# A hybrid decoder layer on one core: where the forget sums are loaded, where a unit's output is stored, when the last stick-breaking sums are reduced, and when the last rows are scaled and turned

## The chip, the core and the metric

The kernel runs on one core of a Trainium2 chip. The metric is the time of one execution on the device, in microseconds (us). The engines of the core are TensorE (PE in the profile, with its weight loads as PEld), VectorE (DVE), ScalarE (ACT), GpSimd (POOL) and SyncE (SP), which here does nothing but issue transfers. Each engine works through its own instructions in the order in which they stand. All data is float32.

## What is computed

One layer of a decoder with a sequence of 2048 and a width of 1024. The rows are normalised and modulated, projected once, and go through 16 heads of width 64: 8 of forgetting attention (FoX) and 8 of stick-breaking attention. Each head's output is normalised, all are projected back, and a gated MLP with a short causal convolution follows.

```python
def forgetting_attention(q, k, v, log_f):
    F = jnp.cumsum(log_f, axis=-1)
    ...
        s = jnp.einsum('bhqd,bhkd->bhqk', q_blk, k) * scale
        s = s + F_blk[..., None] - F[:, :, None, :]
        s = jnp.where(causal, s, -jnp.inf)
        return jnp.einsum('bhqk,bhkd->bhqd', jax.nn.softmax(s, axis=-1), v)

def stick_breaking_attention(q, k, v):
    ...
        log_one_minus_beta = jnp.where(strict, jax.nn.log_sigmoid(-z), 0.0)
        rest = lax.cumsum(log_one_minus_beta, axis=3, reverse=True) - log_one_minus_beta
        a = jnp.where(strict, jnp.exp(jax.nn.log_sigmoid(z) + rest), 0.0)
        return jnp.einsum('bhqk,bhkd->bhqd', a, v)

h = rms_norm(x, g_attn) * (1.0 + scale_a) + shift_a
proj = h @ w_in                       # q, k, v of FoX and of stick-breaking, forget logits
mix = concat([head_rms_norm(o_fox, g_out_fox), head_rms_norm(o_sb, g_out_sb)])
x = x + gate_a * (mix @ w_out)
h = rms_norm(x, g_mlp) * (1.0 + scale_m) + shift_m
u = causal_depthwise_conv(h @ w_up, conv_w, conv_b)
x = x + gate_m * ((silu(u_gate) * u_val) @ w_down)
return rms_norm(x, g_final)
```

## The kernel before

Every float32 operand of a matmul is split into a high and a low part, and each product is made of three matmuls (high by high, high by low, low by high). Most splits are a copy on ACT (L45) and a subtraction (L46) on DVE or, for some, on POOL.

**Units.** Attention is done in 32 units. A unit is a kind (stick-breaking `sb` or FoX `fox`), a pair of heads p from 0 to 3, and a block tb of 512 queries. The 16 units of stick-breaking come first, then the 16 of FoX, in both cases pair by pair and block by block. Inside a unit there are two halves of 256 queries (`j2`), and in each the two heads of the pair. A head makes its logits (L596, L597), turns them into weights, transposes the weights through PE (L606; the copies out are L610 on ACT and L611 on DVE), and multiplies them by V (L615). In stick-breaking the weights come from a scan on DVE (L636), in front of which POOL clears the part over the diagonal (L633).

**FoX and its forget sums.** `fox_head` (L657 to L685) adds the cumulated forget logarithms of the keys to the logits in an operation of DVE that also keeps the smallest value (L675); for the diagonal chunk POOL first makes a masked copy `Fd` (L672). ACT's Exp (L679) then makes the weights and their sum. The sums `Fb` of a head, spread to all partitions, are four tiles of 128 x 1024 for a pair of heads; `load_sums` (L648 to L655) loads them from memory through SP. It runs ahead of unit 14 for pair 0, and with block 0 of each later pair (L1040). The four tiles share four buffers, so a load waits until DVE has done with the sums of the pair before.

**A unit's output.** The parts of the output are added up in `oT` on DVE (L738). `head_var` (L707 to L726) squares each half on POOL (L711) and puts a reduction on a list; the reduction, two small matmuls (L716) and one or two small operations of DVE (L722, L724), is made 13 steps of the program later, by `tick`. At the end of the unit SP stores `oT` to memory, as `os` (L740). Where the program goes from stick-breaking to FoX, `tick(1 << 20)` makes all reductions that are left, since the pool `sx`, in which the squares lie, is closed there (L1036 to L1038).

**Work around the units.** The projections of later pairs are generators, woven into the units step by step. `proj` reads the normalised input `hs` back from memory, 512 KB a tile (L468, on SP), and accumulates on PE (L342, L413). SP also loads Q (L362), K (L363), V (L364) and the weights (L316), and a second generator works on the modulation of the MLP (L776 and following).

**The order.** The program is written in this woven order, and a scheduler then fixes the order of the instructions on each engine when the kernel is built. `tc.issue_after` keeps an instruction behind another one. On the chip, an engine whose next instruction has to wait holds up all that stand behind it.

**The start of the MLP.** The first pair of up-projections is `pair_first` (L1327 to L1345): in each round j it makes seven products (L1316). After round 1 it calls `finish_last` (L1390 to L1394), which finishes the last chunk of rows of the attention output: `scale` multiplies two tiles of 128 rows by their norm (L997, L999), and four `turn_rows` transpose them on PE (L1005, in the bank `bc`) and modulate and store them (ACT, L1013).

## Time and profile before

| | us |
|---|---|
| median of 3 runs | 2949.6 |
| lowest and highest run | 2947.95 and 2951.05 |
| the profiled execution | 2949.67 |
| its span, from the first to the last instruction | 2948.0 |
| PE busy | 2872.7 |
| DVE busy | 2187.3 |
| ACT busy | 1689.3 |
| POOL busy | 899.8 |

The last stick-breaking unit adds its last output at 875.4 us of the span and the last FoX unit at 1519.5; the output projection follows until about 1712, and the MLP to the end. A row of the timeline has the start, the length, the engine, the line and what is written and read; in square brackets stands for how long the engine was idle just before, and what ended it. A row of waits has the sum, the number and the longest. A row of windows has, for each engine, the busy time and the count of instructions, then the clock granted to PE as a share of the full one, the mean busy share of the 16 DMA engines, and GB/s. A row of a line has an operation's least, median and largest length in nanoseconds. An engine's name with a q is its queue, where transfers are issued.

### The profile page before, as it was taken

What the parts mean: (1) busy time and instruction counts of PE and PEld (TensorE: products, weight loads), DVE (VectorE), ACT (ScalarE), POOL (GpSimd) and SP (SyncE); (2) the same over time, 40 slices, a digit from 0 to 9 for tenths busy, and PEclk for the clock granted to TensorE, in tenths of its full rate; (3) what the DMA queues carried; (4) which work ended last, traced back from release to release, by engine and by line L of the source; (5) the groups of instructions that cost most, each with busy time, mean ns of one, the idle gap of its engine ahead of it and who ended that gap; (6) DMA issues with size and microseconds to landing.
All of it is one profiled execution on the core that took longest, in us unless ns stands there. A gap on an engine that the chain in (4) does not pass through costs nothing.

```text
span 2948.0 us, 45934 instructions
## 1 busy us (share of the span) xinstructions
PE 2872.7 (97%) x15772; PEld 2466.9 (84%) x15772; DVE 2187.3 (74%) x3464; ACT 1689.3 (57%) x3187; POOL 899.8 (31%) x967
## 2 busy tenths in 40 slices
PE   8999999999999999999999999999999999999998
PEld 7888898888988889888788788888788888888887
DVE  5787778877877657658843688888998888575576
ACT  5776767777776666658743554444444444543342
POOL 0431312243022423231213344444254543142200
PEclk8999999999999999999999999999999999999999
DMA  9749756867469794794537765554744444975654
GB/s 292 254 133 328 221 196 210 298 202 234 151 217 355 252 296 145 231 323 140 182 115 232 250 219 134 136 136 125 230 134 128 129 133 129 301 266 189 212 159 148
DMA packets 348346, 601.89 MB, mean 204 GB/s; under 512 B 34672, under 2 KB 178800, under 8 KB 348112
## 3 DMA queue, kind: packets, MB, share of 16 engines
q1 hardware_dynamic: 324208, 558.06, 57.5%
q0 software_dynamic: 10880, 20.97, 4.4%
q10 hardware_dynamic: 13024, 19.93, 1.9%
q8 instruction: 124, 2.03, 0.3%
q14 instruction: 110, 0.90, 0.1%
HBM read 420.77 MB, written 177.02 MB: 203 GB/s over the span
## 4 chain that ended last, share of the span: by engine, by line
PE 48%; DVE 2%; DMA 2%; issue 1%; ACT 1%; SPq 0%; POOL 0%; DVEq 0%; ACTq 0%; POOLq 0%
PE ps_o L1316 19%; PE ps_t L1316 7%; PE ps_o L1613 6%; PE ps_t L1613 3%; PE ps_bc L1613 3%; PE ps_o L912 3%; PE ps_pv L615 2%; PE ps_pt L606 1%; PE ps_bc L912 1%; PE ps_qk L596 1%; DMA r<-rstd 1%; PE ps_o L1608 1%; DVE op L46 1%; PE ps_qk L597 1%; DMA hm<-hf_m 1%
## 5 line engine op out<-in xcount | busy, mean ns | idle before, releaser
L1316 PE MATMUL ps_o<-op,wu 128*128 128x512 f32 x2592 | 608.3, 389 | 2.0 <-DVE snap L1367 1.5
L1316 PEld LDWEIGHTS ps_o<-op,wu 128*128 128x128 f32 x2592 | 486.1, 188 | 103.9 <-DVE snap L1367 1.9
L611 DVE TENSOR_TENSOR at<-ps_pt,at 128x512 fp32r<-128x512 f32 (+1 forms) x576 | 365.8, 651 | 99.3 <-ACT at L610 96.8
L636 DVE TENSOR_TENSOR_SCAN a<-r,a 128x512 f32<-128x512 f32 (+2 forms) x320 | 368.7, 1168 | 76.6 <-ACT a L631 40.8
L342 PE MATMUL ps_pj<-hp,w_qk 128*128 128x512 f32 x1512 | 408.4, 401 | 11.0 <-DMA hp<-hs 8.6
L615 PE MATMUL ps_pv<-at,V 128*128 128x256 f32 x2304 | 405.5, 293 | 11.7 <-DVE at L611 4.7
L610 ACT ACTIVATE at<-ps_pt 128x512 fp32r<-128x512 f32 (+1 forms) x576 | 319.3, 576 | 139.2 <-PE ps_pt L606 123.0
L615 PEld LDWEIGHTS ps_pv<-at,V 128*128 128x128 f32 x2304 | 335.5, 191 | 44.9 <-DVE at L611 13.6
L342 PEld LDWEIGHTS ps_pj<-hp,w_qk 128*128 128x128 f32 x1512 | 274.7, 189 | 66.9 <-DMA hp<-hs 11.3
L596 PE MATMUL ps_qk<-K,Q 128*128 128x512 f32 (+2 forms) x640 | 266.8, 418 | 9.9 <-ACT a L631 4.7
L45 ACT ACTIVATE wu<-wuraw 128x512 fp32r<-128x512 f32 x204 | 128.8, 632 | 250.2 <-PE ps_o L1316 194.2
L413 PE MATMUL ps_pj<-w_v,hp 128*128 128x256 f32 (+1 forms) x1536 | 239.9, 290 | 1.3 <-DVE hp L422 0.9
L597 PE MATMUL ps_qk<-K,Q 128*128 128x512 f32 (+2 forms) x640 | 237.1, 372 | 0.0
L1316 PE MATMUL ps_t<-op,wu 128*128 128x512 f32 x888 | 220.5, 389 | 0.6 <-DVE op L46 0.6
L413 PEld LDWEIGHTS ps_pj<-w_v,hp 128*128 128x128 f32 x1536 | 211.7, 191 | 10.2 <-DVE q L373 1.3
L630 ACT ACTIVATE r<-ps_qk 128x512 f32<-128x512 f32 (+2 forms) x320 | 173.0, 541 | 59.7 <-PE ps_qk L597 57.0
L46 DVE TENSOR_TENSOR wu<-wuraw,wu 128x512 fp32r<-128x512 f32 x204 | 191.2, 937 | 18.2 <-ACT wu L45 17.0
L1316 PEld LDWEIGHTS ps_t<-op,wu 128*128 128x128 f32 x888 | 166.6, 188 | 35.6 <-DVE op L46 1.1
L606 PE MATMUL ps_pt<-edge,a 128*128 128x128 f32 x1088 | 186.0, 275 | 7.9 <-DVE a L636 7.4
L1613 PE MATMUL ps_o<-op 128*128 128x512 f32 x840 | 191.5, 389 | 0.0
L679 ACT ACTIVATE p<-p,mn 128x128 f32<-128x128 f32 (+15 forms) x128 | 153.9, 1203 | 56.4 <-DVE mn L675 54.8
L1613 PEld LDWEIGHTS ps_o<-op 128*128 128x128 f32 x840 | 157.7, 188 | 32.7
(338 smaller groups left out, 5215.5 us busy)
## 6 DMA issues: line engine op xcount, KB each, us to landing
hp<-hs SPq DMA_DIRECT2D x224, 512.0 KB
wuraw<-in_w_up_dram SPq DMA_DIRECT2D x80, 512.0 KB
ra<-g SPq DMA_DIRECT2D x136, 256.0 KB
rb<-in_w_down_dram SPq DMA_DIRECT2D x108, 256.0 KB
g<-u SPq DMA_DIRECT2D x80, 256.0 KB
hs<-hp SPq DMA_DIRECT2D x32, 512.0 KB
hp<-in_w_ada_dram SPq DMA_DIRECT2D x32, 512.0 KB
qk_fox<-q SPq DMA_DIRECT2D x32, 512.0 KB
```

Source lines behind the costliest of these rows:

```text
L46: (lo_engine or nc.gpsimd).tensor_sub(lo, src, f(hi))
L342: nc.tensor.matmul(acc, w[kt][:, a, n], h[:, bb], start=kt == 0 and i == 0, stop=kt == KT - 1 and i == 2)
L413: nc.tensor.matmul(av[:, t * width:(t + 1) * width], hts[kt][:, a, tok], w[1][kt][:, bb, 0:width], start=kt == 0 and m == 0, stop=kt == KT ...
L596: nc.tensor.matmul(b[:, :cw], Q[:, hl, 0, qcols], K[:, hl, :cw], start=True, stop=False)
L597: marks.append(nc.tensor.matmul(b[:, :cw], Q[:, hl, 1, qcols], K[:, hl, :cw], start=False, stop=True).ins)
L606: nc.tensor.transpose(b[:, i * P:(i + 1) * P], blk(kts[kk], qi), ident)
L610: copies = [nc.scalar.activation(at[:, 0, lo:], b[:, lo:], AF.Copy).ins, nc.vector.tensor_sub(at[:, 1, lo:], b[:, lo:], f(at[:, 0, lo:])).ins]
L611: nc.vector.tensor_sub(at[:, 1, lo:], b[:, lo:], f(at[:, 0, lo:])).ins]
L615: m = nc.tensor.matmul(o[:, 0:2 * P], V[kt // 4][:, kt % 4, hl, :], rhs, start=first and kk == 0 and w == 0, stop=last and kk == 1 and w == 1)
L636: nc.vector.tensor_tensor_scan(rev, r[:, 0:need][:, ::-1], rev, 0.0 if right[qi] is None else right[qi][:, 0:1], ALU.mult, ALU.add)
L1316: nc.tensor.matmul(b, w[:, p, j], o[:, q], start=first and i == 0, stop=last and i == 2, skip_group_check=True)
L1613: nc.tensor.matmul(b, a[:, p, t * P:(t + 1) * P], w[:, q], start=first and i == 0, stop=last and i == 2, skip_group_check=True)
```

## The change

Four things change; the arithmetic stays the same.

1. **The sums of pairs 1 to 3 are loaded from ACT's queue**, head by head. `load_sums` takes a head and a queue. In the last unit of a pair, behind each head's last Exp, the two tiles of that head are issued for the next pair. So 12 of 16 loads go from SP to ACT; the first four stay on SP, ahead of unit 14.
2. **The outputs of 31 of 32 units are stored from POOL's queue**, right behind the second square; the last one stays on SP.
3. **The flush of the reductions ahead of FoX is gone.** The last stick-breaking unit puts its squares into another pool, and they are reduced 13 steps later, as all others.
4. **`finish_last` is called after each round:** after round 0 it scales, after round 2 it transposes and modulates. Both stood after round 1.

```diff
-    def load_sums(p):
-        sums = [[], []]
+    def load_sums(p, hl, queue=nc.sync):
+        sums = []
         for t in range(0, NTB, 2):
-            for h in range(2):
-                b = px.tile([P, D], F32, name="Fb", tag="xt", bufs=4)
-                nc.sync.dma_start(b, fs[2 * p + h:2 * p + h + 1, t * TB:(t + 2) * TB].to_broadcast([P, D]))
-                sums[h] += [b[:, 0:TB], b[:, TB:D]]
+            b = px.tile([P, D], F32, name="Fb", tag="xt", bufs=4)
+            queue.dma_start(b, fs[2 * p + hl:2 * p + hl + 1, t * TB:(t + 2) * TB].to_broadcast([P, D]))
+            sums += [b[:, 0:TB], b[:, TB:D]]
         return sums
...
-            nc.scalar.activation(a[:, 0:W], a[:, 0:W], AF.Exp, scale=-1.0, bias=mn, accum_out=ls[:, hl, qc + qi:qc + qi + 1])
+            e = nc.scalar.activation(a[:, 0:W], a[:, 0:W], AF.Exp, scale=-1.0, bias=mn,
+                                     accum_out=ls[:, hl, qc + qi:qc + qi + 1])
+            if qi and then is not None:
+                with tc.issue_after(e.ins):
+                    then()
...
-        last_unit = (kind, p, tb) == units[-1]
+        i = units.index((kind, p, tb))
+        last_unit = i == len(units) - 1
...
-            sq = (sx.tile([P, 2 * P], F32, name="sq", bufs=1) if kind == "sb" else
+            sq = (sx.tile([P, 2 * P], F32, name="sq", bufs=1) if kind == "sb" and i < 15 else
                   px.tile([P, TB], F32, name="sq", tag="z", bufs=2)[:, 0:2 * P])
...
+            if j2:
+                (nc.sync if last_unit else nc.gpsimd).dma_start(os_[mp][tb], oT)
...
+                    then = None
+                    if j2 and tb == NTB - 1 and p < 3:
+                        then = lambda hl=hl: sums_of.setdefault(p + 1, []).append(load_sums(p + 1, hl, nc.scalar))
+                    yield from fox_head(j, 2 * j2, hl, Q, K, V, o, Fbs[hl], ls, then)
...
-        nc.sync.dma_start(os_[mp][tb], oT)
...
         if u == ("fox", 0, 0):
-            tick(1 << 20)
             close_pool("sx")
...
-        if i == 14 or (kind == "fox" and tb == 0 and p):
-            Fbs = load_sums(p if kind == "fox" else 0)
+        if i == 14:
+            sums_of[0] = [load_sums(0, hl) for hl in range(2)]
+        if kind == "fox" and tb == 0:
+            Fbs = sums_of[p]
...
-            if j == 1 and after is not None:
-                after()
+            if after is not None:
+                after(j)
...
-    def finish_last():
-        rows_done(NU - 1, 1)
-        ends[NU - 1].scale()
-        for k2 in range(4):
-            turn_rows(NU - 1, k2, bank(psc, "bc", 2))
+    def finish_last(j):
+        if j == 0:
+            rows_done(NU - 1, 1)
+            ends[NU - 1].scale()
+        elif j == 2:
+            for k2 in range(4):
+                turn_rows(NU - 1, k2, bank(psc, "bc", 2))
```

The scheduler orders all of the program anew, so that many instructions of the first three stages stand a few rows earlier or later than before.

PE where stick-breaking goes over to FoX, before (`a` are the weights of stick-breaking, `at` their transposes, `sq` the squares, `p` the weights of FoX):

```order
L606 MATMUL ps_pt<-edge,a 128x128 x4
L615 MATMUL ps_pv<-at,V 128x256 x12
L716 MATMUL ps_pt<-headsel,sq 128x2 x2
L596 MATMUL ps_qk<-K,Q 128x256
L597 MATMUL ps_qk<-K,Q 128x256
L596 MATMUL ps_qk<-K,Q 128x256
L597 MATMUL ps_qk<-K,Q 128x256
L606 MATMUL ps_pt<-edge,p 128x128 x3
```

The same place with the change:

```order
L606 MATMUL ps_pt<-edge,a 128x128 x4
L615 MATMUL ps_pv<-at,V 128x256 x8
L596 MATMUL ps_qk<-K,Q 128x256
L597 MATMUL ps_qk<-K,Q 128x256
L596 MATMUL ps_qk<-K,Q 128x256
L597 MATMUL ps_qk<-K,Q 128x256
L606 MATMUL ps_pt<-edge,p 128x128
L615 MATMUL ps_pv<-at,V 128x256 x3
L606 MATMUL ps_pt<-edge,p 128x128 x2
L596 MATMUL ps_qk<-K,Q 128x384
L597 MATMUL ps_qk<-K,Q 128x384
```

The first logits of FoX now stand between the last products with V of stick-breaking. The two reductions of `sq` (L716, now L723) come 15 rows further on:

```order
L606 MATMUL ps_pt<-edge,p 128x128 x3
L615 MATMUL ps_pv<-at,V 128x256
L606 MATMUL ps_pt<-edge,p 128x128 x4
L615 MATMUL ps_pv<-at,V 128x256 x3
L723 MATMUL ps_pt<-headsel,sq 128x2 x2
L596 MATMUL ps_qk<-K,Q 128x512
```

They stand there behind six pairs of logits (L596 with L597) and the transposes of the first of them.

SP where the second pair of FoX heads goes over to the third, before:

```order
L362 DMA Q<-qk_fox_0_13205 64x1024 x4
L740 DMA os_2_98<-oT 128x512
L653 DMA Fb<-fs 128x1024 x2
L363 DMA K<-qk_fox_1_14178 64x512 x4
L363 DMA K<-qk_fox_2_14948 64x512
L653 DMA Fb<-fs 128x1024
L363 DMA K<-qk_fox_2_14948 64x512
L362 DMA Q<-qk_fox_1_14178 64x1024
L653 DMA Fb<-fs 128x1024
L362 DMA Q<-qk_fox_1_14178 64x1024 x3
```

The same place with the change:

```order
L362 DMA Q<-qk_fox_0_13213 64x1024 x4
L316 DMA raw_qk<-in_w_in_dram 128x2x128
L363 DMA K<-qk_fox_1_14178 64x512 x4
L363 DMA K<-qk_fox_2_14948 64x512 x3
L362 DMA Q<-qk_fox_1_14178 64x1024 x4
L805 DMA gate_m<-hp 128x1024
L363 DMA K<-qk_fox_2_14948 64x512
L468 DMA hp<-hs_7_91 128x1024
```

The store and the four loads of sums are gone from SP. On ACT the loads for the first head of the third pair stand behind the Exp (L678, before L679) of 2048 columns:

```order
L678 ACTIVATE p,ls<-p,mn 128x1920
L610 ACTIVATE at<-ps_pt 128x512 x3
L678 ACTIVATE p,ls<-p,mn 128x2048
L652 DMA Fb<-fs 128x1024
L609 ACTIVATE at<-edge 128x2x128
L652 DMA Fb<-fs 128x1024
L610 ACTIVATE at<-ps_pt 128x384
L610 ACTIVATE at<-ps_pt 128x512 x2
```

Behind them stand the copies out of the transposes (L610). No transfer stands between these rows on ACT before the change.

More of the change, by code (lines that the diff above doesn't have):

```diff
@@ L688 @@
     deferred = []
+    sums_of = {}
     marks = []
@@ L734, in attend @@
                 else:
-                    yield from fox_head(j, 2 * j2, hl, Q, K, V, o, Fbs[hl], ls)
+                    then = None
+                    if j2 and tb == NTB - 1 and p < 3:
+                        then = lambda hl=hl: sums_of.setdefault(p + 1, []).append(load_sums(p + 1, hl, nc.scalar))
+                    yield from fox_head(j, 2 * j2, hl, Q, K, V, o, Fbs[hl], ls, then)
                 o2 = sb.tile([HD, 2 * P], F32, name="o2", bufs=2)
```

2 lines of the change are left out of this document (1 added, 1 removed).

## The prediction

> **What bounds the kernel now.** I read the page first (busy shares), then the windows by stage, the chain's releasers by PE's waits, SP's waits, and last the timelines at the places these name. The windows are cut where the stages end: units of stick-breaking until 875 us, FoX units until 1520, the output projection until 1712, then the MLP.
>
> ```profile
> PE 2872.7 (97%) x15772; PEld 2466.9 (84%) x15772; DVE 2187.3 (74%) x3464; ACT 1689.3 (57%) x3187; POOL 899.8 (31%) x967
> core 0: us, PE busy (x) PEld busy (x) DVE busy (x) ACT busy (x) POOL busy (x), PEclk, DMA share, GB/s
> 117.00:875.00 758.00, 733.92 (x4814) 655.36 (x4813) 603.23 (x792) 553.37 (x1194) 209.66 (x256) 0.99 0.66 221
> 875.00:1520.00 645.00, 626.63 (x4102) 558.11 (x4103) 442.69 (x1136) 424.94 (x811) 182.49 (x259) 0.99 0.68 228
> 1520.00:1712.00 192.00, 187.67 (x865) 152.56 (x864) 95.94 (x159) 90.50 (x190) 53.61 (x60) 0.98 0.69 227
> 1712.00:2520.00 808.00, 805.34 (x3553) 665.73 (x3552) 702.03 (x816) 385.06 (x531) 361.15 (x319) 1.00 0.55 149
> ```
>
> TensorE sets the time: it is busy for 2872.7 of 2948.0 us. The change lies between 117 and about 1705 us, and PE's order of work is unchanged after that. In the first three stages PE is idle for 24.1 + 18.4 + 4.3 = 46.8 us (length less busy, row by row). No rearrangement that leaves the matmuls alone can win more than this and what a throttled clock adds. PE's waits from 117 to 1712 us say what they are:
>
> ```profile
> engine line waited for: us in total, times, longest us
> PE ps_pj L342 <- DMA hp<-hs: 8.6, 6, 3.6
> PE ps_pt L606 <- DVE a L636: 5.7, 12, 1.2
> PE ps_qk L596 <- ACT a L631: 4.7, 6, 1.9
> PE ps_pv L615 <- DVE at L611: 4.7, 12, 0.8
> PE ps_pt L716 <- POOL sq L711: 1.6, 1, 1.6
> PE ps_bc L1005 <- DVE x1u L999: 0.2, 1, 0.2
> ```
>
> The largest is a load: a projection (L342) waits for the normalised input `hs`, read back from memory. The chains inside a head (L606, L596, L615) keep the same distances in the new order, so I leave them at nothing. The loads are issued by SP, whose instructions run in order, and SP itself stands at:
>
> ```profile
> SPq L740 <- DVE oT L738: 84.7, 16, 15.4
> SPq L653 <- DVE mn L675: 35.7, 5, 13.4
> ```
>
> These are the instructions that the change takes off SP: 31 of 32 unit stores (L740), and 12 of 16 forget-sum loads (L653). Their 120 us are no gain by themselves: most of what queues behind them is needed much later.
>
> **The change, part by part.** *The last stick-breaking sums (the flush removed).* At the handover PE's timeline has
>
> ```profile
> start us, us, engine line op out<-in xcount [idle before <-releaser]
> 872.67 1.36 PE L615 MATMUL ps_pv<-at,V 128*128 128x256 f32 x8 [0.21 <-DVE at L611]
> 874.37 0.62 PE L615 MATMUL ps_pv<-at,V 128*128 128x256 f32 x3 [0.34 <-DVE at L611]
> 876.60 1.01 PE L716 MATMUL ps_pt<-headsel,sq 128*128 128x2 f32 x4 [1.61 <-POOL sq L711]
> 878.12 0.55 PE L596 MATMUL ps_qk<-K,Q 128*128 128x256 f32 x1 [0.51 <-PE ps_pt L716]
> ```
>
> The flush makes PE reduce a square that POOL has yet to make, with nothing placed between. In the new order six FoX logit groups and more of their transposes stand ahead of L716, so the 1.61 and 0.51 go, and the last L615 have FoX work between them (0.21 and 0.34): −2.7 in all. The granted clock falls there too:
>
> ```profile
> 869.00:882.60 13.60, 10.93 (x63) 9.81 (x61) 8.66 (x23) 9.51 (x22) 5.48 (x9) 0.75 1.02 316
> 882.60:889.40 6.80, 6.80 (x42) 5.85 (x41) 4.56 (x14) 5.46 (x15) 1.59 (x4) 1.00 1.02 408
> ```
>
> A clock of 0.75 over 13.6 us is 3.4 us less of full speed. If it follows from the idle stretch it goes with it; if not it stays: 0 to −3.4, and I take two thirds, −2.3, since the clock is 1.00 right behind. Sum −5.0 (bounds 0, if the FoX logits wait on loads instead, and −6.1).
>
> *Forget sums off SP.* At pair 0 to 1, SP stands at an L653 and issues an `hs` load late, which PE then waits for:
>
> ```profile
> 1016.35 0.34 SPq L776 DMA_DIRECT2D hp<-in_w_ada_dram  x1
> 1023.69 0.34 SPq L653 DMA_DIRECT2D Fb<-fs  x1
> 1024.60 0.86 SPq L468 DMA_DIRECT2D hp<-hs  x2
> 1031.12 0.97 PE L342 MATMUL ps_pj<-hp,w_qk 128*128 128x512 f32 x3 [2.62 <-DMA hp<-hs]
> ```
>
> From issue to use are 6.5 us. SP was free at 1016.7; without L653 it would issue this load when its buffer comes free, which PE's order puts about 7.4 us of matmuls ahead of the use (estimate: rows counted in the order, each at its line's mean). That covers the 6.5: −2.6 (bounds 0 and −2.6). The same at pair 1 to 2 (SP, PE and ACT in the timeline, then two windows, columns as above):
>
> ```profile
> 1185.77 1.72 SPq L653 DMA_DIRECT2D Fb<-fs  x2
> 1193.80 3.01 SPq L363 DMA_DIRECT2D K<-qk_fox  x5
> 1196.91 0.54 SPq L653 DMA_DIRECT2D Fb<-fs  x1
> 1204.37 0.36 SPq L468 DMA_DIRECT2D hp<-hs  x1
> 1213.01 2.36 PE L342 MATMUL ps_pj<-hp,w_qk 128*128 128x512 f32 x6 [3.60 <-DMA hp<-hs]
> 1188.54 2.00 ACT L679 ACTIVATE p<-p,mn 128x2048 f32<-128x2048 f32 x1
> 1198.00:1214.00 16.00, 12.39 (x97) 11.25 (x96) 10.64 (x28) 9.35 (x20) 2.17 (x5) 0.99 1.01 281
> 1214.00:1218.00 4.00, 4.00 (x19) 3.67 (x18) 1.55 (x3) 3.88 (x11) 1.37 (x2) 0.61 0.87 345
> ```
>
> Here the load takes 8.6 us from issue to use, with the 16 DMA engines full (share 1.01 from 1198 to 1214). On ACT the forget loads go out behind this head's last Exp, at 1190.5: some 5 us later than now, into the same full stretch. In the new order SP's row of this load has the two single Fb rows (0.54 us of issue each) no longer ahead of it, and PE's use stands a little later. I take −1.6 of the 3.6 and half of the 1.6 us that the clock of 0.61 costs in the 4 us after: −2.4 (bounds 0 and −5.2).
>
> The Trainium skill ("DMA: Bandwidth & Descriptors", section "Issuing engines are not separate DMA queues") says that another issuing queue saves the issuer's time only, since all queues run on the same 16 engines; the row with share 1.01 agrees, and by it alone this place would give the issue time, about −1.1, in place of −2.4.
>
> In exchange, uses of `hs` loads elsewhere shift by 20 to 90 PE rows, and at five of them the matmuls between the buffer's release and the use shrink from 6.0–7.5 us to 5.3–5.7, against the 6.5 us above: new waits of 0.8 to 1.2 each, 2.2 to 5 in all, less what SP wins by arriving earlier. I take +1.1 (bounds 0 and +5).
>
> *Their issue from ACT.* The output projection already issues loads from ACT (L1013):
>
> ```profile
> L1013 ACTq DMA_DIRECT2D hm<-hf_m x32: 366/367/417, 1527.0 to 1723.3; - x32
> L1427 POOL DMA_DIRECT2D g<-g x20: 884/900/927, 1758.0 to 2514.3; - x20
> L711 POOL TENSOR_TENSOR sq<-oT x64: 608/615/1641, 99.2 to 1521.7; 128x256 f32<-128x256 f32 x64
> DVE a L636 <- POOL a L633: 29.0, 40, 2.6
> ```
>
> 12 x 0.367 = 4.4 us on an engine that is busy for 425 of 645 us in this stage; behind each load stand the copies L610 that feed PE. Bounds 0 and +4.4; I take +0.5, for ACT's slack.
>
> *Stores from POOL.* 31 x 0.900 (L1427, 256 KB, POOL's own software queue, as are these) = 27.9 us of POOL, busy for 210 of 758 and 182 of 645 us. The store follows the square, whose operand it shares, so it waits for nothing new; behind it stand the diagonal selects (L633, L672) and the hi/lo splits. DVE already waits 29.0 us for L633 (the last row above), so some of the 16 stores in the stick-breaking stage can land on that chain. No row of DVE's waits names FoX's select. Bounds 0 and +27.9; I take one store exposed of 31, +0.9, as POOL is idle for three quarters of the time.
>
> By the Trainium skill ("SBUF — State Buffer", section "SBUF: two separate sides") descriptors of a GpSimd-issued DMA can be locked out by VectorE's operations, some 620 ns alone becoming 3100. L1427 shows no such thing: 884 to 927 with DVE busy for 702 of 808 us.
>
> *Last rows.* Both halves of the scaled rows are ready at 1704.92, and one of eight transposes is 0.19 late:
>
> ```profile
> 1703.15 1.77 DVE L999 TENSOR_SCALAR x1u<-x1u,ss_m 128x1024 f32<-128x1024 f32 x1
> 1704.97 0.33 PE L1005 MATMUL ps_bc<-edge,x1u 128*128 128x128 f32 x1 [0.19 <-DVE x1u L999]
> ```
>
> DVE's order there is unchanged and the transposes stand 7 to 12 matmuls later, so the 0.2 goes: −0.2 (bounds −1, if the first product groups run on better, and +1, if what needs the transposed rows comes late).
>
> *Sum:* −5.0 − 2.6 − 2.4 + 1.1 + 0.5 + 0.9 − 0.2 = −7.7 us. The profiled execution took 2949.67 (span 2948.0, and 1.7 around it), 0.07 over the median of the runs: 2949.67 − 7.7 = 2942.0.
>
> **Rivals.** *Larger gain.* SP's 120 us of standing held more than the two loads I found: all `hs` waits (8.6) go, with the handover's 6.1 and 1.6 of clock at 1214, no new waits appear, and two of the small inner waits shrink with earlier K and Q: 8.6 + 6.1 + 1.6 − 1.4 for the two queues = −14.9, which is 2935 whole and 2938 if a quarter of it fails. For it: the stage has 46.8 us idle. Against it: the DMA engines are full where the waits are.
>
> *The waits only move.* PE's order is fixed when the program is built, and a load still goes out 5 to 7 us ahead of its use; only the handover's idle 2.7 goes, +1.1 for new waits: 2948. For it: the five shorter leads. Against it: SP no longer stands at 1016 to 1023.
>
> *Slower: stores on POOL.* If the store stands ahead of the select that the next head's DVE scan waits for, each costs its 0.9 on the chain scan, transpose, PE. The other terms sum to −8.6, so this decides from ten stores exposed (no gain), and 16 exposed in stick-breaking at 0.9 = 14.4 give +5.8; with all 31, 27.9 − 8.6 = +19. I price it at 2956. For it: 40 waits of DVE for L633, and PE's 12 waits for the scan. Against it: POOL stands idle for three quarters.
>
> *ACT stands at its loads.* An Fb load must wait, by its semaphores, for earlier K loads of SP in some of the six places (the `hs` loads above took 6.5 and 8.6 us); ACT's copies then stop, and PE runs dry after two or three. Two such places at some 5 us of ACT, half exposed, are +5 and spoil the −5.0 of the two `hs` places: 2952.
>
> **How the numbers follow.** About 0.2% (5.9 us) is what a measurement of this kernel can tell from no change, so faster begins under 2943.7. Forecast 0.45 (own range 2938 to 2947; two thirds of it, 0.31, faster, 0.14 the same); larger gain 0.25 (all faster); waits only move 0.10 (the same); POOL 0.12 (slower); ACT 0.08 (half the same, half slower). Faster 0.56, same 0.28, slower 0.16. The range 2934 to 2956 leaves out a tenth of the larger gain and the worse half of POOL's case.
>
> **What would show it.** After: no L716 wait on POOL and no clock under 1.00 near 870–880; no 2.6 us wait for `hs` near 1030, and under 2 us near 1209; SP's waits for oT gone; POOL's stores at 0.9 us with DVE's wait for L633 near 29 us; ACT's longest wait ahead of an Fb load under 1 us; PE's idle time from 117 to 1712 us near 42. If DVE's wait for POOL grows by over 10 us, or PE waits more for L636, POOL's stores were not free; if `hs` waits stand at 8 us or more, the loads only moved; and if the FoX logits wait for K, Q or Fb at the handover, the first term is wrong.

## The result and the profile after

The changed kernel took 2955.48 us (median of 12 executions, 2951.74 to 2963.99); the kernel before took 2949.91 beside it (12 executions). The ratio is 1.0027 with a 95% interval of 1.0017 to 1.0036: 0.27% slower, where 0.26% faster was forecast. The profiled execution of after took 2955.47 us, with a span of 2953.7.

The first row of its page, and then the windows by stage, cut at the same places of PE's work as those of before (columns as there):

```profile
PE 2870.4 (97%) x15772; PEld 2464.2 (83%) x15772; DVE 2174.3 (74%) x3464; ACT 1686.0 (57%) x3187; POOL 911.9 (31%) x998
```

```profile
117.00:880.60 763.60, 734.81 (x4818) 657.25 (x4816) 605.91 (x798) 552.73 (x1197) 213.64 (x271) 0.99 0.66 218
880.60:1528.30 647.70, 626.73 (x4105) 556.59 (x4104) 439.79 (x1133) 424.33 (x813) 190.99 (x275) 0.99 0.69 228
1528.30:1717.50 189.20, 184.79 (x862) 150.18 (x860) 95.76 (x158) 89.33 (x190) 53.68 (x61) 1.00 0.69 229
```

PE is busy about as long as before (2870.4 and 2872.7 us). What grew is its idle time: 28.8 + 21.0 + 4.4 = 54.2 us (length less busy, row by row), against 46.8 before and the 42 forecast. How this splits between the stages is less sure. By these cuts the stick-breaking stage, in which only POOL's stores, and late in it the last reductions, were changed, lost most (+4.7). But the 1.61 us in which PE waited for the last square before stand just behind the cut at 875 us. Cut behind them, stick-breaking lost 3.1 us (25.7 to 28.8) and FoX 4.2 (16.8 to 21.0):

```profile
117.04:876.60 759.56, 733.88 (x4815) 655.35 (x4813) 603.61 (x793) 554.89 (x1196) 210.41 (x257) 0.99 0.66 221
876.60:1520.18 643.58, 626.80 (x4102) 558.25 (x4103) 442.27 (x1135) 423.56 (x810) 181.70 (x257) 0.99 0.68 228
```

One execution of each kernel says little about the split. `only_fin` (below), in which both stages stand in the order of before, has 28.4 and 15.7 us in them, and 46.2 in all three. PE's waits from 100 to 1720 us in after:

```profile
PE ps_pj L342 <- DMA hp<-hs: 13.3, 9, 5.7
PE ps_pt L606 <- DVE a L636: 9.1, 12, 1.8
PE ps_pt L606 <- DVE xm L567: 2.8, 1, 2.8
```

These are rows as in the prediction: the sum, the number and the longest. The wait of L716 for POOL has gone, as it should. But the waits for `hs` rose from 8.6 to 13.3 us, and the chains inside a head, which the prediction left at nothing, rose too: the wait for the scan from 5.7 to 9.1, and a new one of 2.8. Three places show how. The first is SP and PE around 1062 us, in the timeline:

```profile
1037.59 10.85 SPq L363 DMA_DIRECT2D K<-qk_fox  x8
1048.54 2.46 SPq L362 DMA_DIRECT2D Q<-qk_fox  x4
1053.92 5.62 SPq L363 DMA_DIRECT2D K<-qk_fox  x4
1062.39 0.80 SPq L468 DMA_DIRECT2D hp<-hs  x2
1068.11 1.22 PE L342 MATMUL ps_pj<-hp,w_qk 128*128 128x512 f32 x2 [5.67 <-DMA hp<-hs]
1223.39 1.94 PE L342 MATMUL ps_pj<-hp,w_qk 128*128 128x512 f32 x5 [4.14 <-DMA hp<-hs]
```

The 2.62 us near 1028 are gone, as forecast. The new order of SP, however, has an `hs` load behind 16 loads of K and Q. It goes out at 1062.39, when PE has 0.05 us of work left before it needs the tile (1068.11 − 5.67 = 1062.44). The wait that came is about twice the one that went. The last row is the wait at 1209 of before: 4.14 us at 1219, where 3.60 was.

The second place is ACT in the same stretch. Its queue rows and the wait that ends with them:

```profile
1049.25 1.11 ACTq L652 DMA_DIRECT2D Fb<-fs  x2
1050.41 0.40 ACT L678 ACTIVATE p<-p,mn 128x128 f32<-128x128 f32 x1 [3.28 <-DMA K<-qk_fox]
```

ACT does no work for 3.28 us at two sum loads: it stands for 2.12 us until the first goes out (from 1050.41 − 3.28 = 1047.13 to 1049.25), and the issue of the two takes most of the rest. What ends the wait is a transfer of K that no instruction of ACT reads here. In the built program every transfer of SP and ACT uses one of eight completion semaphores (counters that a transfer raises when it has landed) in turn, and waits for the transfer that used it last; in the trace the first of these loads waits on number 109 and then uses 109 itself. With SP busy issuing K, ACT's load waits for a K tile of SP's. No wait of PE follows closely here: the next over 0.7 us is that at 1062. The 16 DMA engines are full (share 1.01) from 1040 to 1068 us:

```profile
1040.00:1068.00 28.00, 22.44 (x153) 20.36 (x151) 15.15 (x41) 17.78 (x41) 8.53 (x14) 0.98 1.01 301
```

So a load that goes out earlier there may do so at the cost of another, which the last experiment takes up.

The third place is at 121 us, where the first store stands on POOL. DVE and POOL in after:

```profile
121.29 6.68 DVE L636 TENSOR_TENSOR_SCAN a<-r,a 128x256 f32<-128x256 f32 x1 [0.63 <-POOL a L633]
120.15 0.79 POOL L718 DMA_DIRECT2D os<-oT  x1
120.94 0.31 POOL L633 TENSOR_SCALAR_AFFINE_SELECT a<-a 128x128 f32<-128x128 f32 x1
121.20 1.28 POOL L46 TENSOR_TENSOR hp<-xm,hp 128x512 fp32r<-128x512 f32 x1
122.43 1.29 POOL L46 TENSOR_TENSOR V<-hp,V 128x512 fp32r<-128x512 f32 x1
123.67 1.29 POOL L46 TENSOR_TENSOR q<-hp,q 128x512 fp32r<-128x512 f32 x1
124.92 2.49 POOL L46 TENSOR_TENSOR hp<-xm,hp 128x512 fp32r<-128x512 f32 x2
128.73 1.12 PE L606 MATMUL ps_pt<-edge,a 128*128 128x128 f32 x4 [2.83 <-DVE xm L567]
```

The store separates two selects, so the second scan starts 0.09 us after POOL has begun five subtractions in a row. The scan ends 0.56 us after the last of them (127.97 and 127.41), at 6.68 us for a form whose mean before is 0.735. PE then waits 2.83. The same place before, POOL and DVE:

```profile
119.67 1.38 POOL L46 TENSOR_TENSOR hp<-xm,hp 128x512 fp32r<-128x512 f32 x1
121.01 1.69 POOL L46 TENSOR_TENSOR V<-hp,V 128x512 fp32r<-128x512 f32 x1
119.90 1.70 DVE L636 TENSOR_TENSOR_SCAN a<-r,a 128x256 f32<-128x256 f32 x1
```

There the same scan followed the first one at once. It began 0.23 us after the first subtraction, so it was held too, but for one subtraction only: it ended 0.55 us after that one (121.60 and 121.05), at 1.70 us. The subtraction behind it took 1.69 instead of 1.29. Why the scan had its turn behind one subtraction here and behind five in after was not tried.

### The profile page after: what moved, and what is told of

Same layout as the page of the kernel before. It is cut to its first block, busy times and chain, and to the rows that moved or that the text cites. A ratio compares the mean times of both kernels' runs of the same rounds, so it can differ in the third digit from the quotient of the medians.

```text
span 2953.7 us, 45920 instructions
## 1 busy us (share of the span) xinstructions
PE 2870.4 (97%) x15772; PEld 2464.2 (83%) x15772; DVE 2174.3 (74%) x3464; ACT 1686.0 (57%) x3187; POOL 911.9 (31%) x998
## 4 chain that ended last, share of the span: by engine, by line
PE 78%; DMA 11%; DVE 4%; issue 3%; ACT 3%; POOL 1%; SPq 1%; ACTq 0%; DVEq 0%; POOLq 0%
PE ps_o L1326 20%; PE ps_pj L342 8%; PE ps_t L1326 8%; PE ps_pv L615 7%; PE ps_o L1625 6%; PE ps_pt L606 6%; PE ps_pj L413 5%; PE ps_t L1625 3%; PE ps_qk L596 3%; PE ps_bc L1625 3%; PE ps_qk L597 3%; DMA hp<-hs 2%; PE ps_o L921 2%; DMA hp<-in_w_ada_dram 1%; DMA r<-rstd 1%
## 5 line engine op out<-in xcount | busy, mean ns | idle before, releaser
L342 PE MATMUL ps_pj<-hp,w_qk 128*128 128x512 f32 x1512 | 414.1, 404 | 14.8 <-DMA hp<-hs 13.3
L615 PE MATMUL ps_pv<-at,V 128*128 128x256 f32 x2304 | 404.2, 292 | 9.9 <-DVE at L611 3.7
L610 ACT ACTIVATE at<-ps_pt 128x512 fp32r<-128x512 f32 (+1 forms) x576 | 318.5, 576 | 139.4 <-PE ps_pt L606 124.9
L615 PEld LDWEIGHTS ps_pv<-at,V 128*128 128x128 f32 x2304 | 335.1, 190 | 43.3 <-DVE at L611 12.7
L596 PE MATMUL ps_qk<-K,Q 128*128 128x512 f32 (+2 forms) x640 | 265.9, 416 | 9.9 <-ACT a L631 4.2
L597 PE MATMUL ps_qk<-K,Q 128*128 128x512 f32 (+2 forms) x640 | 237.0, 371 | 0.0
L413 PE MATMUL ps_pj<-w_v,hp 128*128 128x256 f32 (+1 forms) x1536 | 233.3, 288 | 1.5 <-DVE hp L422 0.9
L606 PE MATMUL ps_pt<-edge,a 128*128 128x128 f32 x1088 | 183.5, 274 | 14.0 <-DVE a L636 10.8
L678 ACT ACTIVATE p<-p,mn 128x128 f32<-128x128 f32 (+15 forms) x128 | 153.8, 1202 | 65.6 <-DVE mn L674 61.9
```

Source lines behind the costliest of these rows:

```text
L342: nc.tensor.matmul(acc, w[kt][:, a, n], h[:, bb], start=kt == 0 and i == 0, stop=kt == KT - 1 and i == 2)
L413: nc.tensor.matmul(av[:, t * width:(t + 1) * width], hts[kt][:, a, tok], w[1][kt][:, bb, 0:width], start=kt == 0 and m == 0, stop=kt == KT ...
L596: nc.tensor.matmul(b[:, :cw], Q[:, hl, 0, qcols], K[:, hl, :cw], start=True, stop=False)
L597: marks.append(nc.tensor.matmul(b[:, :cw], Q[:, hl, 1, qcols], K[:, hl, :cw], start=False, stop=True).ins)
L606: nc.tensor.transpose(b[:, i * P:(i + 1) * P], blk(kts[kk], qi), ident)
L610: copies = [nc.scalar.activation(at[:, 0, lo:], b[:, lo:], AF.Copy).ins, nc.vector.tensor_sub(at[:, 1, lo:], b[:, lo:], f(at[:, 0, lo:])).ins]
```

## The experiments

The arithmetic is that of before in all of them. Times are medians; the difference is to the median of the kernel before on the same chip. The ratio, with its 95% interval, is not simply the quotient of these two medians: where the two columns differ, the ratio and its interval decide.

### One edit at a time

Four kernels, each the kernel before with one of the four edits. The edits are those of the diff in the section on the change: the `os` store behind the second square on POOL (`only_os`), the loads of the sums from ACT (`only_fb`), the flush left out and the last squares in `px` (`only_flush`), `finish_last` after every round (`only_fin`).

> The kernel before with the second edit alone (31 unit stores from POOL). In the built order nothing differs from the kernel before until POOL's row 21 and PE's row 135, near 117 us, so all that the changed kernel lost by 845 us (4.7 us at equal PE work) must be of this edit. Theory A (stores from POOL put POOL's two-input operations at other moments, where they lock a DVE scan out): 4 to 6 us slower than before, with a scan L636 of over 5 us near 121 us, and POOL's stores themselves at about 0.58 us each. Theory B (the loss is made by the sums on ACT): within 1 us of before. The prediction's own rival (POOL's time exposed): DVE's wait for L633 over 39 us.

> The kernel before with the first edit alone (12 of 16 sum loads on ACT). Orders differ only from PE's row 2241, near 1020 us. Theory B (the loads on ACT meet K, Q and hs loads of SP, share their completion semaphores and reorder SP): 3 to 6 us slower than before, with a wait of PE for hs of 4 us or more between 1028 and 1070, and an ACT wait of 2 to 4 us ahead of an Fb load. Theory A: within 1 us, or 2.6 us faster as forecast, with no hs wait over 2 us near 1030.

> The kernel before with the third edit alone (no flush between stick-breaking and FoX). Orders are those of before until PE's row 1912, near 870 us. The prediction: 3 to 5 us faster, no wait of L716 and no clock under 1.00 near 876. Theory C (the wait only moves): within 1 us, the 2.1 us of L716 and L596 coming back as waits of L606 for the Exp of FoX's first rows, behind its table load of 1.28 us on ACT.

> The kernel before with the fourth edit alone (last rows scaled after round 0, turned after round 2). SP's order is that of before throughout; PE's differs only near 1700 us. All theories: within 0.5 us of before, PE's idle time from 1699 to 1710 us 0 to 0.3 us.

| | us | difference | ratio |
|---|---|---|---|
| stores on POOL alone | 2956.75 | +5.6 | 1.0019 (1.0005 to 1.0032) |
| sums on ACT alone | 2955.28 | +4.1 | 1.0021 (1.0012 to 1.0031) |
| no flush alone | 2948.92 | −2.2 | 0.9998 (0.9987 to 1.0009) |
| last rows alone | 2950.80 | −0.4 | 0.9996 (0.9983 to 1.0009) |

So the two moves of transfers each cost time, and the two others can't be told from nothing. `only_flush` shows why the 5.0 us forecast for the handover did not come. PE's, ACT's and SP's timelines in it:

```profile
875.36 0.33 PE L606 MATMUL ps_pt<-edge,p 128*128 128x128 f32 x1 [1.36 <-ACT p L679]
873.51 1.28 ACT L679 ACT_TABLE_LOAD   x1
1049.28 2.22 SPq L468 DMA_DIRECT2D hp<-hs  x3
1056.36 2.92 PE L342 MATMUL ps_pj<-hp,w_qk 128*128 128x512 f32 x6 [5.95 <-DMA hp<-hs]
```

The wait for POOL's square has gone. The first transposes of FoX now stand there, and they wait 1.36 us for ACT's Exp, which first loads its table (1.28). And with no transfer moved to another queue, SP's new order by itself makes a wait of 5.95 us for an `hs` load at 1050.4 (1056.36 − 5.95), just as in after.

### Edits undone, and two together

`no_os` and `no_fb` are the changed kernel with one edit taken back; `flush_fin` is the kernel before with the third and fourth edit.

```diff
 no_os
-            if j2:
-                (nc.sync if last_unit else nc.gpsimd).dma_start(os_[mp][tb], oT)
...
+        nc.sync.dma_start(os_[mp][tb], oT)
 no_fb
-                        then = lambda hl=hl: sums_of.setdefault(p + 1, []).append(load_sums(p + 1, hl, nc.scalar))
...
+        if i == 14 or (kind == "fox" and tb == 0 and p):
+            Fbs = load_sums(p if kind == "fox" else 0)
```

> The changed kernel with the unit stores back on SP (first, third and fourth edit kept). If the stores' move costs what it cost alone: PE's idle time up to 875 us is back at 22 to 27 us (28.8 in the changed kernel), and the time 3 to 6 us under the changed kernel, 0 to 2 us over before.

> The changed kernel with the sums back on SP (second, third and fourth edit kept). If the sums on ACT cost what they cost alone (4 us): 2 to 5 us under the changed kernel. If what one edit costs depends on the order that the others leave, there is no such sum, and the time can lie on either side, up to the 19 us that a single store moved to POOL brought.

> The kernel before with the third and fourth edit, without the two moves of transfers. Both alone stood at or a little below before (0.9998 and 0.9996), so they should add up to 1 to 4 us faster than before, with the 5.9 us wait for hs near 1050 still there (it was there without the sums on ACT). If the two moves are what makes these edits work, it is at or over before.

| | us | difference | ratio |
|---|---|---|---|
| after without POOL's stores | 2949.00 | −2.0 | 0.9994 (0.9981 to 1.0007) |
| after without ACT's sums | 2968.76 | +17.7 | 1.0053 (1.0039 to 1.0068) |
| no flush and last rows | 2947.47 | −4.3 | 0.9991 (0.9980 to 1.0002) |

Taking the stores back wins what after had lost. Taking the sums back, which cost 4.1 us alone, makes the kernel slower by another 12. The edits do not add up, so these runs give no price of one transfer as such.

### Other queues, and part of the stores

```diff
 os_first, os_rest
+            if j2:
+                (nc.gpsimd if (kind, p, tb) == units[0] else nc.sync).dma_start(os_[mp][tb], oT)
...
+                (nc.gpsimd if (kind, p, tb) != units[0] and not last_unit else nc.sync).dma_start(os_[mp][tb], oT)
 os_act
+                (nc.sync if last_unit else nc.scalar).dma_start(os_[mp][tb], oT)
 fb_pool
-                        then = lambda hl=hl: sums_of.setdefault(p + 1, []).append(load_sums(p + 1, hl, nc.scalar))
+                        then = lambda hl=hl: sums_of.setdefault(p + 1, []).append(load_sums(p + 1, hl, nc.gpsimd))
```

> The kernel before with only the first unit's store on POOL; the other 31 stay on SP. If the loss of the second edit is the locked-out scan near 121 us (6.69 us in the run with all 31 stores on POOL, 1.70 before), this one store brings it back: a scan of over 6 us near 120, PE waits of 2.8 and 1.5 us near 123 to 128, a throttled clock at 128 to 132 in some runs, and 3 to 5 us in the end. If the loss is spread over the 31 stores, this run is within 1 us of before. The scheduler reorders much behind this store, so the verdict rests on the first 200 us and on the time alone.

> The kernel before with units 2 to 31 storing from POOL and the first unit from SP (30 stores moved). Order is that of before up to PE's row 555. If the first store's collision is the loss: no scan over 4 us near 121, and the time within 2 us of before. If POOL's issue time or the spread of collisions is the loss: 4 to 6 us slower, as with all 31.

> The kernel before with 31 stores issued from ACT in place of POOL. DVE's order is that of before through all of stick-breaking (first difference at its row 838) and PE's up to row 368, where POOL's stores reordered both from row 135. So SP is relieved as in the changed kernel, and little else moves. If the loss comes from the reordering and POOL's re-timed operations: PE's idle time up to 875 us at 22 to 27 us and the time within 2 us of before. If a store behind SP's queue was needed where it was (transfers colliding once they go out sooner): 3 us or more over before.

> The first edit alone, but with the 12 loads issued from POOL's software queue in place of ACT. If the loss of that edit is ACT standing 2.0 us at its load until a K load of SP has landed, and the Exp rows behind it (waits of 1.2 and 0.8 us of L606), it goes: no such ACT wait, no L606 wait over 0.6 us at 1070 to 1090, and 2 to 4 us faster than the run with ACT. If the loss is that these loads meet the hs loads on full DMA engines, it stays at 3 to 4 us over before.

| | us | difference | ratio |
|---|---|---|---|
| first store alone on POOL | 2970.41 | +18.7 | 1.0067 (1.0055 to 1.0079) |
| stores of units 2 to 31 on POOL | 2955.06 | +3.3 | 1.0016 (1.0004 to 1.0027) |
| 31 stores from ACT | 2972.67 | +21.6 | 1.0068 (1.0052 to 1.0084) |
| 12 sum loads from POOL | 2954.85 | +3.1 | 1.0019 (1.0008 to 1.0029) |

The long scan at 121 us (6.69 us) is there with the first store alone and not with the other thirty, but one store costs more than thirty. The thirty have a held scan of their own, 4.37 us at 177 us behind the second unit's store. So how long a scan is held, real as it is, does not decide the time by itself. Nor does ACT's standing decide the loss of the sums: with them on POOL's queue ACT stands at none, and most of the loss stays (+3.1 against +4.1). In `os_act` the standing is plain. At the handover ACT waits before a store until an `hs` load of SP has landed, and PE behind it:

```profile
888.56 1.28 ACT L679 ACT_TABLE_LOAD   x1 [11.26 <-DMA hp<-hs]
890.40 1.18 PE L606 MATMUL ps_pt<-edge,p 128*128 128x128 f32 x3 [9.74 <-ACT p L679]
```

### Controls: a new order, and no transfer moved

The kernel before, with the reductions of the squares made 12 or 14 steps later instead of 13. All transfers stay on their queues; the scheduler makes a new order.

```diff
-            deferred.append([reduce, 13])
+            deferred.append([reduce, 12])
...
+            deferred.append([reduce, 14])
```

> A control that moves no transfer: the kernel before with reductions deferred by 12 steps in place of 13, which makes the scheduler reorder attention from PE's row 153 on. If reordering alone can cost what the two moves cost: 2 to 8 us over before, with PE's idle time in the two attention stages up from 42 us by that amount. If it takes the stores on POOL: within 1.5 us of before.

> A second control that moves no transfer to another queue: the reductions of the squares are made 14 steps later instead of 13 (12 in the first control, which came out at 1.0072). Theory 1 (a new order of all instructions has by itself a price of either sign, by where loads and uses fall against each other): some other ratio, anywhere from 0.996 to 1.008, by waits of PE for loads at other places than before. Theory 2 (only the earlier reduction cost time in the first control, and an order as such costs nothing): within 0.1% of before, or faster, as the reductions come later still, with the waits of before at 1028, 1209 and the handover.

| | us | difference | ratio |
|---|---|---|---|
| 12 steps | 2973.55 | +22.5 | 1.0072 (1.0058 to 1.0086) |
| 14 steps | 2976.92 | +23.7 | 1.0082 (1.0068 to 1.0095) |

Both controls lose three to four times what the change lost, the first far more than was expected of it. The stretch that took 1595.18 us before (117.04 to 1712.22, first row) takes, at the same work of PE, 20.5 us more with 12 steps and 23.2 more with 14:

```profile
117.04:1712.22 1595.18, 1548.40 (x9779) 1366.20 (x9778) 1142.05 (x2087) 1068.99 (x2195) 445.94 (x574) 0.99 0.67 224
115.99:1731.66 1615.67, 1555.38 (x9779) 1370.26 (x9778) 1136.82 (x2087) 1068.47 (x2195) 439.89 (x574) 0.99 0.67 221
115.65:1734.01 1618.36, 1559.97 (x9779) 1371.27 (x9778) 1145.22 (x2087) 1069.39 (x2195) 442.01 (x574) 0.98 0.67 221
```

PE is idle in it for 46.8 us before, 60.3 with 12 steps and 58.4 with 14, and busy for 7.0 and 11.6 us longer. So a third to a half of the loss in this stretch is not waiting but a longer busy time of PE; the mean granted clock of the whole execution is 0.988 and 0.986, against 0.990 before. Why the clock falls more often there no run shows. Of the waits, the two lines that grew in after grew here too, with 14 steps and then with 12:

```profile
PE ps_pj L342 <- DMA hp<-hs: 14.0, 12, 5.4
PE ps_pt L606 <- DVE a L636: 12.9, 17, 1.7
PE ps_pj L342 <- DMA hp<-hs: 11.7, 9, 6.9
PE ps_pt L606 <- DVE a L636: 9.3, 15, 1.3
```

So such waits can come with an order alone. They are no proof of a new order, though: with the attention in the order of before they are 9.7 and 6.1 us in `only_fin`, and 11.6 and 8.5 in `pin_os` of the next section, which moves the stores. That both controls lose, on either side of 13, shows that the order of before lies better than these two; why its fits are so good was not looked into.

### The order held

An added function ties each instruction to the one that stands before it on its engine in a recorded order, so that the scheduler has no choice. In `pin_os` the 31 stores go to POOL behind the second square and all else stands as before. `pin_fb` does the same for the 12 loads on ACT. `pin_os_order` is the reverse: the order that was made for the stores on POOL, with the stores back on SP.

```diff
+def _pin(nc, tc):
+    by = {i.name: i for i in nc.cur_bb.bb.instructions}
+    for seq in _order():
+        prev = None
+        for k in seq:
+            i = by.get(f"I-{k}")
...
+                tc.add_manual_dep(i, prev.name, mybir.DependencyInfo(mybir.DependencyClass.NoSync, mybir.DependencyReason.DATA), reason="order")
+            prev = i
...
         tile_trunk_kernel(tc, *args)
+        _pin(nc, tc)
```

> The 31 stores on POOL, each right behind its unit's second square, with every other instruction of all engines held in the order of the kernel before (written out by hand; PE's, DVE's and ACT's orders are equal row by row). Theory O (what cost time was the order that the scheduler made anew): within 1.5 us of before, PE's idle time up to 875 us at 22 to 27 us. Theory M (a store on POOL costs time by itself): 3 to 6 us over before, as with the scheduler's own order (5.6).

> The 12 sum loads on ACT, two behind the last Exp of each head, with every other instruction held in the order of the kernel before. Theory O: within 1.5 us of before, or up to 2.6 us faster if the hs wait near 1028 goes as the prediction had it (SP no longer stands at a sum load). Theory M (ACT standing at its loads for a completion semaphore costs PE time): 3 us or more over before, with an ACT wait of 2 us or more ahead of a load and waits of L606 for the Exp behind it.

> The counterpart: PE, DVE, ACT and POOL in the order that the scheduler made for stores on POOL, but the stores back on SP, each behind the SP instruction that it follows in the kernel before. Theory O: 3 to 7 us over before, PE's idle time up to 875 us at 27 us or more. Theory M: within 1.5 us of before.

| | us | difference | ratio |
|---|---|---|---|
| 31 stores on POOL, order of before | 2953.10 | +1.8 | 1.0007 (0.9993 to 1.0021) |
| 12 sums on ACT, order of before | 2952.57 | +1.3 | 1.0006 (0.9993 to 1.0020) |
| order of the stores on POOL, stores on SP | 2960.06 | +8.8 | 1.0035 (1.0020 to 1.0050) |

With the order held, neither move can be told from no change; the 5.6 and 4.1 us that the two moves cost alone fall to 1.8 and 1.3. The intervals overlap, so these runs don't prove how the 5.6 and 4.1 divide. For the stores, PE's idle time points the same way. The stretch of the controls (46.8 us idle before) in `only_os` and in `pin_os`:

```profile
115.26:1716.56 1601.30, 1546.70 (x9779) 1363.46 (x9778) 1141.05 (x2087) 1067.49 (x2195) 458.18 (x605) 0.99 0.67 223
119.91:1716.53 1596.62, 1548.16 (x9780) 1365.05 (x9779) 1145.49 (x2087) 1068.04 (x2195) 460.36 (x605) 0.99 0.67 224
```

It is 54.6 us with the scheduler's order and 48.5 with the order held. For the sums it is 48.7 and 47.9, too close to tell. The kernel before with its order held and nothing moved was not run, so what the added ties do by themselves is not known apart. Even with the order held a store holds up a scan: the one at the first store takes 1.70 us as before, but one behind the second unit's store, at 175.40, takes 4.29, beside four of POOL's two-input operations.

`pin_fb` shows what is won and what is given back, in the waits of ACT and PE from 875 to 1530 us and in their timelines:

```profile
ACT p L679 <- DMA K<-qk_fox: 5.9, 1, 5.9
PE ps_pj L342 <- DMA hp<-hs: 5.9, 4, 3.5
```

```profile
1031.23 0.96 PE L342 MATMUL ps_pj<-hp,w_qk 128*128 128x512 f32 x3 [0.56 <-DMA hp<-hs]
1055.48 0.39 PE L596 MATMUL ps_qk<-K,Q 128*128 128x256 f32 x1 [1.00 <-DVE mn L675]
1073.02 1.33 ACT L783 ACTIVATE hp<-hp,cs 128x512 f32<-128x512 f32 x2 [6.65 <-DMA hp<-in_w_ada_dram]
1075.00 0.90 PE L606 MATMUL ps_pt<-edge,p 128*128 128x128 f32 x3 [2.85 <-ACT p L679]
1218.32 2.08 PE L342 MATMUL ps_pj<-hp,w_qk 128*128 128x512 f32 x4 [3.49 <-DMA hp<-hs]
```

The `hs` wait near 1028 shrinks from 2.62 to 0.56 and all of them in the stage from 8.4 to 5.9. ACT does no work for 5.9 us at its loads, their issue included, from 1047.88 on (1053.74 − 5.86 in its timeline); the one wait of PE right behind it is the 1.00 at 1054.5. Then, some 20 us on, ACT waits 6.65 us for a load of `in_w_ada` (4.3 at most before), and PE 2.85 for the Exp behind it. So what was won on one load went along with new waits at others; whether ACT's standing made the second one late is open. `pin_os_order` is no clean counterpart. Two waits of PE in it, 3.64 us at 495 and 5.54 at 548, are not in `only_os`, whose order of PE and DVE it has. In both ACT, and PE behind it, waits for POOL's work on values that are read back through SP (`xt`, L458); some 20 us ahead of the second, SP stood for 6.8 us at one of the stores put back on it. The two add up to 9.2 us, more than the 8.8 that this run lost, so it speaks neither for the order nor against it. It does show that the long scan at 121 us needs the store as well as the order: without the store the scan takes 1.71 us here, and with the store in the order of before 1.70 (`pin_os`).

### A version meant to be faster

`best` has the third and fourth edit, its own order held, and on SP the three `hs` loads that came late in `only_flush` moved ahead of 16 loads of K and Q. The order stands in the kernel as a list of numbers; in words the edit to it is:

```diff
 L468 DMA hp<-hs on SP, three rows
-    behind 12 rows L363 and 4 rows L362
+    ahead of them
```

> Third and fourth edit without the two moves, in the order that the scheduler made for them, with one correction by hand on SP: the hs loads 5, 6 and 7 of FoX's second projection stand ahead of 16 K and Q loads in place of behind them (their buffers are free by 1027 us, and they were issued at 1051). The 5.9 us wait of PE near 1050 goes: 5 to 9 us faster than before, 1 to 5 us faster than without the correction. If the K and Q loads that now come later are missed instead, it stays at 0 to 4 us faster.

It took 2948.27 us, −3.0, at a ratio of 0.9990 (0.9977 to 1.0004): no better than `flush_fin`. The `hs` wait at 1050 has gone. The next load in the line is late instead, again one of `in_w_ada` that ACT needs, and PE stands as long as in `only_flush`, 8 us further on:

```profile
1062.18 1.33 ACT L782 ACTIVATE hp<-hp,cs 128x512 f32<-128x512 f32 x2 [7.38 <-DMA hp<-in_w_ada_dram]
1064.78 1.12 PE L606 MATMUL ps_pt<-edge,p 128*128 128x128 f32 x4 [5.89 <-DVE at L611]
```

No kernel tried is clearly faster than the one before.

## Why the prediction was wrong

**The step that failed** is the one sentence "The chains inside a head (L606, L596, L615) keep the same distances in the new order, so I leave them at nothing", and with it the search for new waits, which went no further than `hs` loads. The prediction priced each moved transfer by what it takes on an engine, and the loads by the two places where SP had been seen late. But the scheduler had moved many instructions of all engines, and PE's waits come from how closely a load or a chain ends before its use. In after the waits for the scan, put at nothing, grew by 3.4 us, a new one of 2.8 came, and those for `hs` grew by 4.7 where 3.1 were to go (2.6 and 1.6, less 1.1 of new ones). That a new order can have a price of its own, and a large one, the controls show: +22.5 and +23.7 us with no transfer moved. How much of the +5.6 is this price is not proven; with the order held the two moves cost 1.8 and 1.3 us, neither of which can be told from nothing.

That 2955.48 lies just inside the stated range of 2934 to 2956 is luck: the upper end came from the rival "stores on POOL", whose mechanism is not what happened.

**Handover, −5.0.** Measured alone −2.2 by the medians and almost nothing by the ratio (0.9998), within the noise. The 1.61 went, as predicted. But in after 1.53 us for the scan and 1.25 for the Exp of FoX stand there in its place, and the clock falls there too, if for less long:

```profile
870.99 0.44 PE L606 MATMUL ps_pt<-edge,a 128*128 128x128 f32 x2 [1.53 <-DVE a L636]
882.24 0.33 PE L606 MATMUL ps_pt<-edge,p 128*128 128x128 f32 x1 [1.25 <-ACT p L678]
```

```profile
873.00:880.00 7.00, 7.00 (x39) 6.18 (x37) 5.98 (x12) 2.48 (x6) 1.69 (x2) 0.79 1.02 243
```

The 2.3 us for the clock were read from one execution, and no run shows that the fall goes with the flush. In `only_flush` the clock is 1.00 from 866 to 880 us, but it is 0.50 just ahead of that:

```profile
859.20:866.00 6.80, 6.32 (x20) 5.18 (x21) 5.21 (x8) 4.26 (x11) 1.78 (x2) 0.50 0.97 364
```

From 855 to 895 us it is 0.91 both in before and in `only_flush`, and 0.96 in `only_fin`, which has the flush and the order of before. What was won in `only_flush` is met by the `hs` wait of 5.95 us.

**The `hs` waits, −2.6 and −2.4.** The first was right as a mechanism, and with the order held 2.1 of its 2.6 us came. The second did not come: 4.14 and 3.49 us remain where 3.60 was. The `hs` load of that place now takes 11.7 us from issue to use (1223.39 − 1211.70), against 8.6 before:

```profile
1211.70 0.60 SPq L468 DMA_DIRECT2D hp<-hs  x1
```

The load went out 7.55 us ahead of the point where PE needed it, against 5.04 before; what this issue won, the transfer took back. The rule weighed there in the prediction (the Trainium skill, "DMA: Bandwidth & Descriptors", section "Issuing engines are not separate DMA queues": another queue saves the issue alone) was nearer than the 2.4, since with the order held the place won 0.1. **New `hs` waits, +1.1:** under-sized. Of the 13.3 us in after, 5.67 are a single wait that the counted distances did not show, since they took each load as issued on time.

**ACT's issue, +0.5.** The rows of the 12 loads:

```profile
L652 ACTq DMA_DIRECT2D Fb<-fs x12: 326/334/612, 1028.3 to 1377.8; - x12
```

The issue takes 0.334 us, a little less than the 0.367 assumed. The standing of the rival "ACT stands at its loads" is there, 3.28 us in after and 5.9 with the order held, some 5 us at a place as that rival had it. But PE shows no wait behind the first and 1.00 close behind the second: there half exposed was too much. Whether +0.5 was right no run shows apart.

**POOL's stores, +0.9.** The store's rows:

```profile
L718 POOL DMA_DIRECT2D os<-oT x31: 568/580/786, 120.2 to 1467.0; - x31
```

The issue takes 0.58 us, less than the 0.900 assumed. DVE's wait for POOL's select hardly grew (30.1 before and 31.2 after, from 100 to 890 us). So the rival "stores on POOL", at 2956, had the time nearly right, but not by the mechanism that it named: no 16 stores of 0.9 stand on the chain. The runs point to the order made around the stores (5.6 us alone, 1.8 with the order held), without proving it.

**Last rows, −0.2.** −0.4 within the noise: not contradicted.

**The rival "the waits only move"** was nearest to what happened. It was priced at 2948, since it let the handover's idle time go and took the moved waits to be no longer than the old ones. What stays open is how the +5.6 us of after divide between the places: the edits do not add up, and executions of one kernel spread by 5 to 10 us to either side.

## What to carry to other kernels

When an edit makes a scheduler order the program anew, price the order first: compare where each load goes out and where it is used over the whole program, not only at the places that were slow, and take a control that only perturbs the order as the measure of what a new order may do (here 0.7 to 0.8%). To learn what a moved transfer itself costs, hold the order fixed, and run the held order with nothing moved beside it. Read the granted clock next to the waits, and in more than one execution. Where the DMA engines are full, a load made earlier may make the next one late, so look for the next one before counting the gain.

## What the hardware showed that was not expected

A scan of DVE can be held for the whole length of a train of POOL's two-input operations: 6.68 us beside a mean of 0.735, while POOL's five subtractions ran at 1.25 to 1.29 each. It need not be: before, the same scan began behind the first of these subtractions too, and was held for that one alone (1.70 us). The Trainium skill ("SBUF — State Buffer", section "SBUF: two separate sides") says that the two share a pair of ports, and that whoever starts first has it for the whole instruction. The trace agrees, and adds that the loser may or may not get its turn between POOL's instructions.

ACT did no work for 3.3, 5.9 and 11.3 us at its own transfers (in after, `pin_fb` and `os_act`), most of it standing until a transfer of SP had landed whose data ACT did not need. A queue of one's own does not make a transfer independent here: the transfers of SP and ACT share eight completion semaphores.
